# Splitting every second weight tile by DMA and ScalarE, in a two-layer decoder trunk

## The chip, the cores and the metric

The kernel runs on one core of a Trainium2 chip, as one program. The metric is the device time of one execution in microseconds (us), taken as the median over runs.

## The reference

Two residual layers over 256 positions of width 2048, in float32, each behind an RMSNorm, and a final RMSNorm:

```python
def even_mixer(h, w_in, ..., w_out):
    proj = h @ w_in
    ...
    return jnp.concatenate([y_a, y_b], axis=-1) @ w_out

def odd_mixer(h, w_in, ..., w_out, lambda_init):
    proj = h @ w_in
    q, k, v, g = jnp.split(proj, 4, axis=-1)
    ...
    return o @ w_out

def reference(x, norm_w, ..., final_norm_w):
    h = x
    for layer in range(DEPTH):
        hn = rmsnorm(h, norm_w[layer])
        if layer % 2 == 0:
            h = h + even_mixer(hn, ...)
        else:
            h = h + odd_mixer(hn, ...)
    return rmsnorm(h, final_norm_w)
```

In layer 0 the projection feeds a state-space scan (y_a) and a gated mixing of positions (y_b); in layer 1 it feeds differential attention with a gate.

Four weight matrices make nearly all of the work: the input projections of both layers (2048 x 12320 and 2048 x 16384) and their output projections (4096 x 2048 each).

## The kernel before, in words

The matrices lie in memory as tiles of 128 partitions x 2048 float32 (1 MB), in the order of their use. TensorE multiplies in float32r, a float32 with fewer bits, so each float32 operand is kept as a high part (the value as float32r) and a low part (the rest), and a product is made of three: high by high, high by low, low by high. Activations (`xw`, `ya`, `yb`) are split once. Weights are split as they arrive, in half tiles of 128 x 1024.

The path of a weight tile before: `fetch` (line 122) loads it whole into one of three `raw` buffers, by a DMA that SyncE issues (line 124). `halves` (127) splits it in two by `split` (115): ScalarE copies half of it into a `wh` tile (line 118), VectorE subtracts that from the raw half into a `wl` tile (line 119). The pool `wp` has three buffers for each of `raw`, `wh` and `wl`. Tiles are used in one of two ways. `t_accum` (141), through `t_half` (132), has the weight as the stationary operand: eight pairs of matmuls per half, line 136 with `wh` (512 columns) and line 138 with `wl` (256 columns). `tok_proj` (157) has it as the moving operand: four triples per half, lines 168 (`wh`), 169 (`wl`) and 170 (`wh`). The last block of the last output projection is written out apart (line 529).

Layer 0 goes through eight state-space groups (tiles B, C and two x each, and four z tiles for every two groups), four v blocks of four tiles, and sixteen pairs of u and zb tiles (the gating part). `out_proj` takes two tiles, a and b, for each of 16 blocks; per block ScalarE copies half the sum out of PSUM (`sm`), squares the result (`sq`), and POOL adds the square to a running sum `sqa` (line 545). Layer 1 goes eight times through eight q and k tiles, four v and four g tiles, with scores and attention between; POOL's row for `rr_h` (line 177) stands once per head.

The program is written in this order, and a planner with a cost table of its own then puts the instructions of each engine into a fixed sequence; an engine executes its sequence strictly in order, and an instruction that waits holds up all behind it. The first two tiles are fetched and split apart from the others (`first_half`, `split_first`). POOL issues a few transfers of its own: constants at the start and, in the gating part, four times the tiles `lw`, `lb`, `ws_j` and `sb_j` of 256 KB (lines 472 to 486).

Of the kernel before, what the change touches and what calls it, by code (L numbers as in the profile page):

```python
# [9 lines left out]
F32 = mybir.dt.float32  # L10
F32R = mybir.dt.float32r
AF = mybir.ActivationFunctionType
ALU = mybir.AluOpType
AX = mybir.AxisListType
# [3 lines left out]
P = 128  # L18
S = 256
D = 2048  # L20
KB = D // P
EPS = 1e-6
# [6 lines left out]


def order_l0():
    """Weight tiles of the first projection, in the order of their use."""
    out = []
    for gp in range(4):
        for g in (2 * gp, 2 * gp + 1):
            out.append(("T", 4096 + g * P))
            out.append(("T", 5120 + g * P))
            out.append(("T", 2048 + 2 * g * P))
            out.append(("T", 2048 + (2 * g + 1) * P))
        for kq in range(4):  # L40
            out.append(("K", gp * 512, kq))
    for vg in range(4):
        for kq in range(4):
            out.append(("K", 10272 + vg * 512, kq))
    for j in range(16):
        out.append(("T", 8224 + j * P))
        out.append(("T", 6176 + j * P))
    return out
# [24 lines left out]
def hybrid_trunk(ctx: ExitStack, tc: tile.TileContext, xT, cols, dskip, dtp, lnw, lnb, sgub, wsT,  # L73
                 wdt, w0, wo0, w1, wo1, outT):
    nc = tc.nc
    v, act, pe, pool = nc.vector, nc.scalar, nc.tensor, nc.gpsimd

    const = ctx.enter_context(tc.tile_pool(name="const", bufs=1))
    wp = ctx.enter_context(tc.tile_pool(name="wp", bufs=3))
    ev = ctx.enter_context(tc.tile_pool(name="ev", bufs=2))  # L80
    big = ctx.enter_context(tc.tile_pool(name="big", bufs=1))
    acc_p = ctx.enter_context(tc.tile_pool(name="acc_p", bufs=4, space=PSUM))
# [3 lines left out]
    def aux(name):  # L86
        return aux_p.tile([P, 512], F32, tag="aux", name=name)

# [1 line left out]
    col = const.tile([P, N_COLS], F32, name="col")  # L90
    act.dma_start(col, cols)
    ident = const.tile([P, P], F32, name="ident")
# [16 lines left out]
    def c1(i):  # L109
        return col[:, i:i + 1]  # L110

# [1 line left out]
    last_split = [None, None]  # L113

    def split(raw, shape, nm):
        wh = wp.tile([P] + shape, F32R, tag="wh", name=f"wh_{nm}")
        wl = wp.tile([P] + shape, F32R, tag="wl", name=f"wl_{nm}")
        last_split[0] = act.activation(wh, raw, AF.Copy).ins  # L118
        last_split[1] = v.tensor_tensor(wl, raw, wh.bitcast(F32), op=ALU.subtract).ins  # L119
        return wh, wl  # L120

    def fetch(src, nm):
        raw = wp.tile([P, 2048], F32, tag="raw", name=f"raw_{nm}")
        nc.sync.dma_start(raw, src)
        return raw

    def halves(src, inner, nm):
        raw = fetch(src, nm).rearrange("p (a b) -> p a b", b=inner)
        n = 2048 // inner // 2
        return [split(raw[:, h * n:(h + 1) * n, :], [n, inner], f"{nm}_{h}") for h in range(2)]  # L130

    def t_half(ps, hv, x, half, first, last):
        wh, wl = hv
# [5 lines left out]
                      start=False, stop=last and k == 15)  # L139

    def t_accum(ps, src, x, first, last, nm):
        """ps[:, :256] += wh.xh ; ps[:, 256:] += wh.xl + wl.xh, over 16 blocks of k."""
        hv = halves(src, P, nm)
        for half in range(2):
            t_half(ps, hv[half], x, half, first, last)
# [25 lines left out]
        return ps  # L171

    def pow_mhalf(dst, ssum, n, scale, nm):
        """dst = (ssum * scale + EPS) ** -0.5 for [P, n]."""
        ms = ev.tile([P, 2], F32, tag="ms", name=f"ms_{nm}")
        v.tensor_scalar(ms[:, :n], ssum, scale, EPS, op0=ALU.mult, op1=ALU.add)
        pool.tensor_tensor(dst, ms[:, :n], mhalf[:, :n], op=ALU.pow)

    def token_rstd(sqs, nm, copy=True):
        """From sums of squares by channel-partition [P, S], in parts: rstd by token, as columns and as rows."""  # L180
        pcs = [aux(f"pc{tb}_{nm}") for tb in range(2)]
        ms = ev.tile([P, 2], F32, tag="ms", name=f"ms_{nm}")
        for tb in range(2):
            for i, sq in enumerate(sqs):
                pe.matmul(pcs[tb][:, 0:1], lhsT=sq[:, tb * P:(tb + 1) * P], rhs=ones[:, 0:1],
                          start=i == 0, stop=i == len(sqs) - 1)
            v.tensor_scalar(ms[:, tb:tb + 1], pcs[tb][:, 0:1], 1.0 / D, EPS, op0=ALU.mult, op1=ALU.add)
        rt = const.tile([P, 2], F32, tag="rt", name=f"rt_{nm}", bufs=2)
        pool.tensor_tensor(rt, ms, mhalf, op=ALU.pow)
        pb = aux(f"pb_{nm}")  # L190
        for tb in range(2):
            pe.matmul(pb[:, tb * P:(tb + 1) * P], lhsT=rt[:, tb:tb + 1].broadcast_to([P, P]),
                      rhs=ident, start=True, stop=True)
        if not copy:
            return rt, pb[:, 0:S]
        rb = const.tile([P, S], F32, tag="rb", name=f"rb_{nm}", bufs=1)
        act.activation(rb, pb[:, 0:S], AF.Copy)
        return rt, rb

    def put_split(dst, src, scale):  # L200
        """dst [P, 2, S] = hi and lo part of src * scale."""
        act.activation(dst[:, 0, :], src, AF.Copy, scale=scale)
        v.scalar_tensor_tensor(dst[:, 1, :], src, scale, dst[:, 0, :].bitcast(F32),
                               op0=ALU.mult, op1=ALU.subtract)

    # ================= layer 0 =================
    with ExitStack() as l0:
        s1 = l0.enter_context(tc.tile_pool(name="ssd1", bufs=1))

        sqs = s1.tile([P, S], F32, name="sqs")  # L210
        # the first two weight tiles come in halves, between the parts of x
        first = [[None, [None, None]] for _ in range(2)]

        def first_half(i, half):
            if half == 0:
                first[i][0] = wp.tile([P, 2048], F32, tag="raw", name=f"raw_first{i}")
            nc.sync.dma_start(first[i][0][:, half * 1024:(half + 1) * 1024], w0[i][:, half * 1024:(half + 1) * 1024])

        def split_first(i, half):
            raw = first[i][0][:, half * 1024:(half + 1) * 1024].rearrange("p (a b) -> p a b", b=P)  # L220
            first[i][1][half] = split(raw, [8, P], f"first{i}_{half}")

        with tc.tile_pool(name="start", bufs=4) as st:
# [35 lines left out]
            pool.tensor_tensor(sqs, sq[:, 0, 0, :], sq[:, 0, 1, :], op=ALU.add)  # L259
            rt0, rb0 = token_rstd([sqs], "n0")  # L260

            # dt and its cumulative decay
            H = 32
            lo = s1.tile([H, 512], F32, name="dt_lo")
            act.activation(lo, pdt[32:64, :], AF.Copy)
# [9 lines left out]
            e = s1.tile(tok, F32, name="dt_e")  # L275
            q = s1.tile(tok, F32, name="dt_q")
# [5 lines left out]
                                       op0=ALU.mult, op1=ALU.add)  # L282
            v.scalar_tensor_tensor(e, z, -1.0, z, op0=ALU.mult, op1=ALU.max)
            act.activation(e, e, AF.Exp, scale=-1.0)
            # log(1 + e) = 2 atanh(e / (2 + e)), e in [0, 1]
            v.tensor_scalar(w, e, 2.0, None, op0=ALU.add)
            v.reciprocal(w, w)
            pool.tensor_tensor(w, e, w, op=ALU.mult)
# [58 lines left out]
        def ssd_group(g):  # L347
            n = f"g{g}"
# [23 lines left out]
            for b in range(2):  # L372
                for c in range(2):
# [4 lines left out]
            pool.memset(xd[:, 2 * S:2 * S + 64], 0.0)  # L378
            v.tensor_tensor(xd[:, 0:2 * S].rearrange("p (c r q) -> p c r q", r=4, q=64), heads(xt),
                            bc(dtk[:, :, hs].rearrange("p c (r o) -> p c r o", o=1), [P, 2, 4, 64]), op=ALU.mult)  # L380
            # carried state of chunk 0 and what it adds to chunk 1
            wt = sp.tile([P, 4], F32, tag="wt", name=f"wt_{n}")
            v.tensor_tensor(wt, csb[:, :, P - 1:P].rearrange("p r o -> p (r o)"), csk[:, 0, hs], op=ALU.subtract)
            act.activation(wt, wt, AF.Exp)
# [60 lines left out]
    with ExitStack() as l0b:  # L445
# [10 lines left out]
        v.tensor_reduce(nmu, vs, axis=AX.X, op=ALU.add)  # L456
        v.tensor_scalar(nmu, nmu, -1.0 / D, None, op0=ALU.mult)
        vq = g1.tile([P, 2], F32, name="vq")
        for tb in range(2):
            junk = gp_.tile([P, D], F32, tag="junk", name=f"vjunk{tb}", bufs=1)  # L460
            act.activation(junk, vt[:, tb, :], AF.Square, bias=nmu[:, tb:tb + 1], accum_out=vq[:, tb:tb + 1])
        vr = g1.tile([P, 2], F32, name="vr")
        pow_mhalf(vr, vq, 2, 1.0 / D, "ln")
        ws_t = sb_t = None
        for j in range(16):
            n = f"j{j}"
# [42 lines left out]
            act.activation(yb[:, j, 0, :], mx, AF.Copy)  # L509
            v.tensor_tensor(yb[:, j, 1, :], mx, yb[:, j, 0, :].bitcast(F32), op=ALU.subtract)  # L510

# [1 line left out]
    resp = ctx.enter_context(tc.tile_pool(name="resp", bufs=1, reuse_waits="tile"))  # L513
    res = resp.tile([P, KB, S], F32, name="res")
    sqa = resp.tile([P, S], F32, name="sqa")

    def out_proj(w, nm, after):
        """res += the projection; the sums of squares of res by channel-partition are left in
        two parts: all blocks but the last, and the last."""
        pool.memset(sqa, 0.0)  # L520
        for n in range(16):
            ps = acc(f"{nm}_{n}")
# [27 lines left out]
    sqp = out_proj(wo0, "o0", lambda n: put_split(xw[:, n], res[:, n, :], c1(C_NW1 + n)))  # L550
    rt1, rb1 = token_rstd(sqp, "n1")

    # ================= layer 1 =================
    with ExitStack() as l1:
        ap = l1.enter_context(tc.tile_pool(name="att", bufs=2, reuse_waits="tile"))
        a1 = l1.enter_context(tc.tile_pool(name="att1", bufs=1, reuse_waits="tile"))
# [16 lines left out]
        wi[0] = 0  # L573

        def qk_block(tag, c0, nm):
            """[d, token] in float32, and tokens from c0 on in hi and lo parts."""
            ps = acc(nm)
            t_accum(ps, nxt(w1), xw, True, True, nm)
            t = t_sum(ps, nm)
            o = ap.tile([P, S], F32, tag=tag, name=nm)  # L580
            v.tensor_tensor(o, t, rb1, op=ALU.mult)
            hl = ap.tile([P, 2, S - c0], F32R, tag=tag + "hl", name=f"{nm}_hl")
            act.activation(hl[:, 0, :], o[:, c0:S], AF.Copy)
            v.tensor_tensor(hl[:, 1, :], o[:, c0:S], hl[:, 0, :].bitcast(F32), op=ALU.subtract)
            return o, hl

        def scores(qs, ks, nm):
            """softmax over both maps of one head, combined and turned: attnT [k, q]."""
            e = ap.tile([P, 768], F32, tag="e", name=f"e_{nm}", bufs=1)
            e0 = e[:, 0:256].rearrange("p (j k) -> p j k", k=P)  # L590
            e1 = e[:, 256:768].rearrange("p (j k) -> p j k", k=S)
# [89 lines left out]
    n = 0  # L681
# [70 lines left out]
```

## Time and profile before

| | |
|---|---|
| median of two runs | 1737.49 us (1736.93 and 1738.04) |
| the profiled execution, first to last instruction (span) | 1735.4 us |
| TensorE busy | 1713.9 us, 99% |
| VectorE, ScalarE, POOL busy | 65%, 57%, 6% |
| mean granted TensorE clock | 0.997 of full speed |
| moved by DMA | 318.68 MB, 184 GB/s |

The profiled execution has no time of its own beside its span; it is 1.5 and 2.6 us shorter than the two runs, which also count what lies around the instructions. Engines: PE is TensorE, DVE is VectorE, ACT is ScalarE, POOL is GpSimd, SP is SyncE, which only issues DMAs here. "Busy" of PE counts a matmul from its start to its modelled end, and matmuls overlap: their pace is read from the distance of their starts. A row of waits names the waiting instruction and, behind the arrow, what released it.

### The profile page before, as it was taken

To read this page: it belongs to the slowest core of one execution; us is meant where nothing else is said; L and a number is where in the kernel's file an instruction comes from. 1 tells how busy PE (TensorE), PEld (TensorE's weight loads), DVE (VectorE), ACT (ScalarE), POOL (GpSimd) and SP (SyncE) were. 2 spreads that over 40 slices of the span, in tenths; PEclk is the share of its full clock that TensorE was granted. 3 is DMA by queue.
4 is the path that set the end of the run, shared out by engine and by line. 5 is a ranking of instruction groups with operands and counts; after the bars stand their busy time and mean duration, and the time that the engine had idled before them with its cause. 6 is when DMAs were issued, how large, how long until landed. Compare 5 with 4: busy or idle time off the path is not lost.

```text
span 1735.4 us, 23829 instructions
## 1 busy us (share of the span) xinstructions
PE 1713.9 (99%) x9232; PEld 1465.9 (84%) x9232; DVE 1128.1 (65%) x1704; ACT 989.3 (57%) x1521; POOL 104.6 (6%) x159
## 2 busy tenths in 40 slices
PE   7999999999999999999999999999999999999997
PEld 6888888888888888888888888888888888888886
DVE  6987878545777655556666565756576665655454
ACT  6776776545777744445455555555554555555443
POOL 3200000100000011110000000000000000001111
PEclk9999999999999999999999999999999999999998
DMA  7645444655555565554445444554545455445552
GB/s 251 211 168 192 176 172 154 227 186 205 196 201 175 184 232 191 194 188 176 170 171 190 173 170 173 182 179 170 184 162 189 170 187 178 170 170 194 194 188 104
DMA packets 46290, 318.68 MB, mean 184 GB/s; under 512 B 5280, under 2 KB 5584, under 8 KB 9440
## 3 DMA queue, kind: packets, MB, share of 16 engines
q1 hardware_dynamic: 44400, 310.30, 50.5%
q0 software_dynamic: 1344, 4.24, 0.9%
q10 hardware_dynamic: 432, 2.61, 0.4%
q8 instruction: 72, 1.18, 0.3%
q14 instruction: 42, 0.34, 0.1%
HBM read 315.00 MB, written 2.13 MB: 183 GB/s over the span
## 4 chain that ended last, share of the span: by engine, by line
PE 96%; DVE 1%; issue 1%; POOL 1%; DMA 0%; ACT 0%; SPq 0%; DVEq 0%; POOLq 0%
PE acc_o L136 13%; PE acc_q L136 7%; PE acc_k L136 7%; PE acc_o L138 7%; PE acc_v L168 5%; PE acc_v L170 5%; PE acc_v L169 5%; PE acc_q L138 3%; PE acc_k L138 3%; PE acc_g L169 3%; PE acc_g L168 3%; PE acc_zb L136 3%; PE acc_u L136 3%; PE acc_g L170 3%; PE acc_x L136 3%; PE acc_zb L138 2%
## 5 line engine op out<-in xcount | busy, mean ns | idle before, releaser
L136 PE MATMUL acc_q<-xw,wh_q 128*128 128x512 f32 x512 | 182.9, 394 | 0.0
L136 PE MATMUL acc_k<-xw,wh_k 128*128 128x512 f32 x512 | 181.5, 395 | 0.0
L118 ACT ACTIVATE wh_v<-raw_v 128x1024 fp32r<-128x1024 f32 x96 | 101.8, 1060 | 125.0 <-PE acc_v L170 83.6
L119 DVE TENSOR_TENSOR wl_v<-raw_v,wh_v 128x1024 fp32r<-128x1024 f32 x96 | 117.5, 1224 | 79.9 <-ACT wh_v L118 79.9
L169 PE MATMUL acc_v<-wl_v,xw 128*128 128x512 f32 x384 | 152.2, 396 | 0.0
L170 PE MATMUL acc_v<-wh_v,xw 128*128 128x512 f32 x384 | 152.2, 396 | 0.0
L138 PE MATMUL acc_k<-xw,wl_k 128*128 128x256 f32 x512 | 145.5, 284 | 0.0
L138 PE MATMUL acc_q<-xw,wl_q 128*128 128x256 f32 x512 | 145.2, 284 | 0.0
L168 PE MATMUL acc_v<-wh_v,xw 128*128 128x512 f32 x384 | 140.4, 397 | 0.0
L119 DVE TENSOR_TENSOR wl_g<-raw_g,wh_g 128x1024 fp32r<-128x1024 f32 x64 | 78.5, 1226 | 78.7 <-ACT wh_g L118 78.7
L119 DVE TENSOR_TENSOR wl_q<-raw_q,wh_q 128x1024 fp32r<-128x1024 f32 x64 | 78.4, 1226 | 61.9 <-ACT wh_q L118 61.9
L118 ACT ACTIVATE wh_q<-raw_q 128x1024 fp32r<-128x1024 f32 x64 | 67.8, 1060 | 83.9 <-PE acc_g L170 23.9
L136 PEld LDWEIGHTS acc_k<-xw,wh_k 128*128 128x128 f32 x512 | 96.4, 188 | 21.3
L118 ACT ACTIVATE wh_g<-raw_g 128x1024 fp32r<-128x1024 f32 x64 | 67.8, 1059 | 80.7 <-PE acc_g L170 53.4
L136 PEld LDWEIGHTS acc_q<-xw,wh_q 128*128 128x128 f32 x512 | 96.4, 188 | 20.2
L118 ACT ACTIVATE wh_k<-raw_k 128x1024 fp32r<-128x1024 f32 x64 | 67.6, 1057 | 75.0 <-PE acc_q L136 49.0
L169 PE MATMUL acc_g<-wl_g,xw 128*128 128x512 f32 x256 | 101.4, 396 | 0.0
L170 PE MATMUL acc_g<-wh_g,xw 128*128 128x512 f32 x256 | 101.0, 395 | 0.0
L119 DVE TENSOR_TENSOR wl_k<-raw_k,wh_k 128x1024 fp32r<-128x1024 f32 x64 | 78.1, 1221 | 34.7 <-ACT wh_k L118 34.7
L138 PEld LDWEIGHTS acc_k<-xw,wl_k 128*128 128x128 f32 x512 | 96.0, 188 | 1.2
L138 PEld LDWEIGHTS acc_q<-xw,wl_q 128*128 128x128 f32 x512 | 96.1, 188 | 0.9
L136 PE MATMUL acc_x<-xw,wh_x 128*128 128x512 f32 x256 | 92.2, 399 | 0.0
(500 smaller groups left out, 4635.6 us busy)
## 6 DMA issues: line engine op xcount, KB each, us to landing
raw_v<-in_w_dram SPq DMA_DIRECT2D x48, 1024.0 KB, 4.8
raw_q<-in_w_dram SPq DMA_DIRECT2D x32, 1024.0 KB, 4.7
raw_k<-in_w_dram SPq DMA_DIRECT2D x32, 1024.0 KB, 4.8
raw_g<-in_w_dram SPq DMA_DIRECT2D x32, 1024.0 KB, 4.8
raw_x<-in_w_dram SPq DMA_DIRECT2D x16, 1024.0 KB, 4.8
raw_z<-in_w_dram SPq DMA_DIRECT2D x16, 1024.0 KB, 4.8
raw_u<-in_w_dram SPq DMA_DIRECT2D x16, 1024.0 KB, 4.8
raw_zb<-in_w_dram SPq DMA_DIRECT2D x16, 1024.0 KB, 4.8
```

The source lines that it names most:

```text
L118: last_split[0] = act.activation(wh, raw, AF.Copy).ins
L119: last_split[1] = v.tensor_tensor(wl, raw, wh.bitcast(F32), op=ALU.subtract).ins
L136: pe.matmul(ps, lhsT=wh[:, i, :], rhs=x[:, k, :, :].rearrange("p a b -> p (a b)"), start=first and k == 0, stop=False)
L138: pe.matmul(ps[:, 256:512], lhsT=wl[:, i, :], rhs=x[:, k, 0, :], start=False, stop=last and k == 15)
L168: pe.matmul(ps[tb], lhsT=xh, rhs=wh, start=k == 0, stop=False)
L169: pe.matmul(ps[tb], lhsT=xh, rhs=wl, start=False, stop=False)
L170: pe.matmul(ps[tb], lhsT=xl, rhs=wh, start=False, stop=k == 15)
```

## The change

From the 42nd tile on, every second weight tile takes another path (`split_by_dma`). It is not loaded raw. POOL issues a DMA that writes the high part straight from memory, casting float32 to float32r; ScalarE writes the negative of the high part into the low tile; POOL issues a second DMA that reads the same weights from memory again and adds them to the low tile. VectorE has no part in it. The other tiles keep their path, but are loaded by halves into raw buffers of half the size. `wp` has four buffers for each of `raw`, `wh` and `wl`. Comments are gone, and two squares of 2048 columns are taken in four of 1024.

```diff
-    wp = ctx.enter_context(tc.tile_pool(name="wp", bufs=3))
+    wp = ctx.enter_context(tc.tile_pool(name="wp", bufs=4))
...
+    def split_by_dma(src, inner, nm):
+        shape = [P, 1024 // inner, inner]
+        wh = wp.tile(shape, F32R, tag="wh", name=f"wh_{nm}")
+        wl = wp.tile(shape, F32R, tag="wl", name=f"wl_{nm}")
+        pool.dma_start(wh.rearrange("p a b -> p (a b)"), src)
+        act.activation(wl, wh.bitcast(F32), AF.Copy, scale=-1.0)
+        pool.dma_start(wl.rearrange("p a b -> p (a b)"), src, accum_op=ALU.add)
+        return wh, wl
+
     def fetch(src, nm):
-        raw = wp.tile([P, 2048], F32, tag="raw", name=f"raw_{nm}")
+        raw = wp.tile([P, 1024], F32, tag="raw", name=f"raw_{nm}")
         nc.sync.dma_start(raw, src)
         return raw
 
+    n_tiles = [0]
+
     def halves(src, inner, nm):
-        raw = fetch(src, nm).rearrange("p (a b) -> p a b", b=inner)
-        n = 2048 // inner // 2
-        return [split(raw[:, h * n:(h + 1) * n, :], [n, inner], f"{nm}_{h}") for h in range(2)]
+        n_tiles[0] += 1
+        by_dma = n_tiles[0] > 40 and n_tiles[0] % 2 == 0
+        out = []
+        for h in range(2):
+            part = src[:, h * 1024:(h + 1) * 1024]
+            if by_dma:
+                out.append(split_by_dma(part, inner, f"{nm}_{h}"))
+                continue
+            raw = fetch(part, f"{nm}_{h}").rearrange("p (a b) -> p a b", b=inner)
+            out.append(split(raw, [1024 // inner, inner], f"{nm}_{h}"))
+        return out
...
-            junk = gp_.tile([P, D], F32, tag="junk", name=f"vjunk{tb}", bufs=1)
-            act.activation(junk, vt[:, tb, :], AF.Square, bias=nmu[:, tb:tb + 1], accum_out=vq[:, tb:tb + 1])
+            for h in range(2):
+                junk = gp_.tile([P, 1024], F32, tag="junk", name=f"vjunk{tb}{h}", bufs=1)
+                act.activation(junk, vt[:, tb, h * 1024:(h + 1) * 1024], AF.Square, bias=nmu[:, tb:tb + 1],
+                               accum_out=vqs[:, tb, h:h + 1])
+        v.tensor_reduce(vq, vqs, axis=AX.X, op=ALU.add)
```

In the changed kernel the lines are 128 (casting DMA), 129 (negation), 130 (adding DMA), 118 and 119 (the old split), 157 and 159 (the pair of matmuls), 562 (`sm`), 566 (`sq`) and 568 (`sqa`). The planner makes a new sequence. ScalarE before, in the first output projection, from block 5 on (`wh_o0_5a_0` is the first half of block 5's tile a, `xw` the split of a finished block):

```order
L118 ACTIVATE wh_o0_5a_0_6162<-raw_o0_5a_6160 128x1024 [waits DMAHW5_49,PE_49,Activation_49]
L118 ACTIVATE wh_o0_5a_1_6166<-raw_o0_5a_6160 128x1024 [waits PE_49,Activation_49]
L118 ACTIVATE wh_o0_5b_0_6204<-raw_o0_5b_6202 128x1024 [waits DMAHW6_49,DVE_49,PE_49]
L539 ACTIVATE sm_o0_4_6150<-acc_o0_4_6065 128x256 [waits PE_49]
L118 ACTIVATE wh_o0_5b_1_6208<-raw_o0_5b_6202 128x1024 [waits DVE_49,PE_49]
L543 ACTIVATE sq_o0_4_6154<-res_5685 128x256 [waits DVE_49,Pool_49]
L202 ACTIVATE xw_92<-res_5685,col_75 128x256
L118 ACTIVATE wh_o0_6a_0_6256<-raw_o0_6a_6254 128x1024 [waits DMAHW7_49,PE_49,Activation_49]
```

ScalarE there now, from the negation for block 4's tile b on:

```order
L129 ACTIVATE wl_o0_4b_0_6261<-wh_o0_4b_0_6260 128x1024 [waits DMASW5_49,DMASW6_49,DVE_49,PE_49]
L118 ACTIVATE wh_o0_5a_0_6314<-raw_o0_5a_0_6312 128x1024 [waits DMAHW5_49,DVE_49,PE_49]
L129 ACTIVATE wl_o0_4b_1_6266<-wh_o0_4b_1_6265 128x1024 [waits DMASW7_49,DMASW4_49]
L118 ACTIVATE wh_o0_5a_1_6320<-raw_o0_5a_1_6318 128x1024 [waits DMAHW6_49,PE_49,Activation_49]
L562 ACTIVATE sm_o0_3_6206<-acc_o0_3_6119 128x256 [waits PE_49]
L566 ACTIVATE sq_o0_3_6210<-res_5827 128x256 [waits DVE_49,Pool_49]
L223 ACTIVATE xw_92<-res_5827,col_75 128x256
L129 ACTIVATE wl_o0_5b_0_6357<-wh_o0_5b_0_6356 128x1024 [waits DMASW2_49,PE_49]
L129 ACTIVATE wl_o0_5b_1_6362<-wh_o0_5b_1_6361 128x1024 [waits DMASW0_49,DMASW3_49,PE_49,Activation_49]
L118 ACTIVATE wh_o0_6a_0_6410<-raw_o0_6a_0_6408 128x1024 [waits DMAHW7_49,PE_49,Activation_49]
```

Every high part was a copy that waited for SyncE's load (`DMAHW`) and a free buffer; now the rows for tile b are negations of line 129 that wait for POOL's transfer (`DMASW`), and the copies for the next tile a stand behind them.

POOL had in this place one row per block, the sum of line 545. Of the difference on POOL, the stretch from block 4's tile b to block 5's:

```order
+L128 DMA wh_o0_4b_0_6260<-in_wo0_dram 128x1024 [waits DVE_49,PE_49]
+L128 DMA wh_o0_4b_1_6265<-in_wo0_dram 128x1024 [waits DMASW2_49,PE_49]
+L130 DMA wl_o0_4b_0_6261<-in_wo0_dram 128x1024 [waits Activation_49]
+L130 DMA wl_o0_4b_1_6266<-in_wo0_dram 128x1024 [waits DMASW4_49,PE_49,Activation_49]
+L128 DMA wh_o0_5b_0_6356<-in_wo0_dram 128x1024 [waits DVE_49,PE_49]
+L568 TENSOR_TENSOR sqa_5828<-sqa_5828,sq_o0_3_6210 128x256 [waits Activation_49,Pool_49]
+L128 DMA wh_o0_5b_1_6361<-in_wo0_dram 128x1024 [waits DMASW6_49,DMASW3_49,PE_49]
+L130 DMA wl_o0_5b_0_6357<-in_wo0_dram 128x1024 [waits Activation_49]
+L130 DMA wl_o0_5b_1_6362<-in_wo0_dram 128x1024 [waits DMASW5_49,DMASW0_49,Activation_49]
```

POOL now issues four transfers per tile b; the first high half waits for TensorE to free its buffer, both low halves wait for ScalarE's negation, and the sum of block 3 stands between two high halves.

## Rows read from the trace of the kernel before

**Rows 1.** The page: busy us (share of the span), by engine.

```profile
span 1735.4 us, 23829 instructions
...
PE 1713.9 (99%) x9232; PEld 1465.9 (84%) x9232; DVE 1128.1 (65%) x1704; ACT 989.3 (57%) x1521; POOL 104.6 (6%) x159
```

**Rows 2.** TensorE's waits (us, times, longest us): two of five.

```profile
PE acc_dt L243 <- DVE wd L239: 8.0, 1, 8.0
PE acc_x L138 <- DVE wl_x L119: 2.8, 2, 1.7
```

**Rows 3.** Timeline of TensorE (start us, us), where two tiles meet.

```profile
1254.66 0.39 PE L168 MATMUL acc_g<-wh_g,xw 128*128 128x512 f32 x1
...
1255.35 0.40 PE L136 MATMUL acc_q<-xw,wh_q 128*128 128x512 f32 x1
...
1255.71 0.40 PE L136 MATMUL acc_q<-xw,wh_q 128*128 128x512 f32 x1
```

**Rows 4.** The page: split of a half tile (busy us, mean ns).

```profile
L118 ACT ACTIVATE wh_v<-raw_v 128x1024 fp32r<-128x1024 f32 x96 | 101.8, 1060 | 125.0 <-PE acc_v L170 83.6
L119 DVE TENSOR_TENSOR wl_v<-raw_v,wh_v 128x1024 fp32r<-128x1024 f32 x96 | 117.5, 1224 | 79.9 <-ACT wh_v L118 79.9
```

**Rows 5.** POOL's transfers: KB, median us to landing; extremes (lw, sb_j); one alone.

```profile
lw<-in_lnw_dram POOLq DMA_DIRECT2D x4, 256.0 KB, 4.9
lb<-in_lnb_dram POOLq DMA_DIRECT2D x4, 256.0 KB, 6.0
ws_j<-in_wsT_dram POOLq DMA_DIRECT2D x4, 256.0 KB, 5.5
sb_j<-in_sgub_dram POOLq DMA_DIRECT2D x4, 256.0 KB, 5.6
...
DMA to landing us min/median/max: 3.6/4.9/5.9
...
DMA to landing us min/median/max: 3.4/5.6/8.3
...
439.66 0.54 POOL L482 DMA_DIRECT2D ws_j<-in_wsT_dram  x1 [12.95 <-PE pm_j L501]
443.87 1.16 POOL L483 TENSOR_SCALAR_AFFINE_SELECT ws_j<-ws_j 128x512 f32<-128x512 f32 x1 [3.67 <-DMA ws_j<-in_wsT_dram]
```

**Rows 6.** SyncE's transfers: KB each, median us to landing.

```profile
raw_q<-in_w_dram SPq DMA_DIRECT2D x32, 1024.0 KB, 4.7
csb_g<-csd SPq DMA_DIRECT2D x8, 512.0 KB, 3.6
```

**Rows 7.** Steps of the gating part, layer 1, the output projection.

```profile
L501 PE MATMUL pm_j<-ws_j,vt x64: 270/275/275, 428.7 to 599.0; 128*128 128x128 f32 x64
...
1337.19 0.69 POOL L177 TENSOR_TENSOR rr_h<-ms_h,mhalf 128x2 f32<-128x2 f32 x1 [73.49 <-DVE ms_h L176]
...
1432.71 0.69 POOL L177 TENSOR_TENSOR rr_h<-ms_h,mhalf 128x2 f32<-128x2 f32 x1 [73.50 <-DVE ms_h L176]
...
1693.47 1.41 POOL L545 TENSOR_TENSOR sqa<-sqa,sq_o 128x256 f32<-128x256 f32 x1 [9.76 <-ACT sq_o L543]
1704.64 1.41 POOL L545 TENSOR_TENSOR sqa<-sqa,sq_o 128x256 f32<-128x256 f32 x1 [9.76 <-ACT sq_o L543]
```

**Rows 8.** Windows (us, busy by engine, PEclk, DMA share, GB/s); a stall.

```profile
30.00:40.00 10.00, 8.89 (x53) 7.80 (x54) 7.00 (x10) 2.58 (x4) 3.54 (x7) 1.00 0.60 210
1722.00:1723.00 1.00, 1.00 (x12) 1.00 (x10) 0.08 (x1) 0.00 (x0) 0.00 (x0) 1.00 0.00 0
1725.00:1726.00 1.00, 0.46 (x2) 0.46 (x3) 0.00 (x0) 0.00 (x0) 0.49 (x1) 0.62 0.00 0
1726.00:1727.00 1.00, 0.77 (x4) 0.47 (x3) 0.19 (x1) 0.00 (x0) 0.00 (x0) 0.50 0.00 0
...
31.11 0.38 PE L138 MATMUL acc_x<-xw,wl_x 128*128 128x256 f32 x1 [1.66 <-DVE wl_x L119]
```

**Rows 9.** The page, SyncE's DMA queue: packets, MB, share.

```profile
q1 hardware_dynamic: 44400, 310.30, 50.5%
```

More of the change, by code (lines that the diff above doesn't have):

```diff
@@ L210, in hybrid_trunk @@
         sqs = s1.tile([P, S], F32, name="sqs")
-        first = [[None, [None, None]] for _ in range(2)]
+        first = [[[None, None], [None, None]] for _ in range(2)]
         def first_half(i, half):
-            if half == 0:
-                first[i][0] = wp.tile([P, 2048], F32, tag="raw", name=f"raw_first{i}")
-            nc.sync.dma_start(first[i][0][:, half * 1024:(half + 1) * 1024], w0[i][:, half * 1024:(half + 1) * 1024])
+            first[i][0][half] = fetch(w0[i][:, half * 1024:(half + 1) * 1024], f"first{i}_{half}")
         def split_first(i, half):
-            raw = first[i][0][:, half * 1024:(half + 1) * 1024].rearrange("p (a b) -> p a b", b=P)
+            raw = first[i][0][half].rearrange("p (a b) -> p a b", b=P)
             first[i][1][half] = split(raw, [8, P], f"first{i}_{half}")
@@ L458, in hybrid_trunk @@
         vq = g1.tile([P, 2], F32, name="vq")
+        vqs = g1.tile([P, 2, 2], F32, name="vqs")
         for tb in range(2):
-            junk = gp_.tile([P, D], F32, tag="junk", name=f"vjunk{tb}", bufs=1)
-            act.activation(junk, vt[:, tb, :], AF.Square, bias=nmu[:, tb:tb + 1], accum_out=vq[:, tb:tb + 1])
+            for h in range(2):
[3 more added lines that the diff above has]
+        v.tensor_reduce(vq, vqs, axis=AX.X, op=ALU.add)
         vr = g1.tile([P, 2], F32, name="vr")
```

## The prediction

> **What bounds the kernel now.** I read the page's shares first: TensorE is busy 1713.9 of 1735.4 us, VectorE 65% [rows 1]. The list of what TensorE waited for is next: five waits, the longest 8.0 us in the start-up and 2.8 us for a low part of a weight tile, 13 us together [rows 2]. Nothing that relieves another engine can therefore give back 2% (35 us), about what a measurement of this kernel can tell from no change. The question is only whether the new path delivers its tiles in time.
>
> Its deadline comes from TensorE's pace. A pair of lines 136 and 138 starts every 0.35 us (1255.35 to 1255.71), a triple of lines 168 to 170 every 0.69 us [rows 3]. Half a weight tile (1024 columns) is eight pairs or four triples, so 2.8 us in either kind. Half tiles rotate through four buffers for the high and four for the low part. From the changed tiles on, the four belong in turn to a tile split on VectorE (two halves) and one split by DMA (two halves). When TensorE lets go of a half split by DMA, it has three more halves to do, 3 x 2.8 = 8.4 us, before it needs the next content of that buffer. I call one VectorE tile plus one DMA tile a pair of tiles. It takes 95.52 / 8 = 11.94 us in layer 1 (one POOL row per 16 tiles), 11.17 us in the output projections, and (599.0 - 428.7) / 15 = 11.36 us in the gating part [rows 7].
>
> **The change part by part.** Tiles are counted by the code: of 286 tiles the even ones above 40 go by DMA, 123 tiles or 246 halves: 27 in the rest of layer 0's input projection, 32 in the output projections, 64 in layer 1.
>
> VectorE loses 246 subtractions of 1.224 us [rows 4], 301 us. It ended only 2.8 us of TensorE's waits, so I count 0.
>
> ScalarE makes a negation of 128 x 1024 where it made a copy of 128 x 1024, 1.06 us each [rows 4]: 0 in busy time. But the negation waits in an in-order queue for a DMA. Behind it on ScalarE stand the high part of the next VectorE tile and the PSUM copies, as the order rows show. At 1.06 us each they have room inside the cycle below.
>
> POOL gets 492 transfers. By the order rows a tile's four stand as high 0, high 1, low 0, low 1, and each low part waits for its negation.
>
> The chain per buffer is the cost: TensorE frees the buffer, DMA for the high part, negation, adding DMA for the low part, eight pairs on TensorE, and only then is the buffer free again. No reordering shortens this loop, so a pair of tiles cannot take less than the sum of the four.
>
> - *High part, 512 KB from POOL.* The trace has no such transfer. Sixteen of 256 KB from POOL have medians by tensor of 4.9 to 6.0 us from issue to landing; the quickest are 3.4 and 3.6, the slowest, in a batch of eight, 8.3; one on its own was waited for 3.67 us after its issue of 0.54 [rows 5]. From 512 KB to 1024 KB SyncE's loads go from 3.6 to 4.7 us, so 0.6 us for 256 KB more [rows 6]. That gives 4.8 for a lone transfer and 6.1 for the median. Three transfers of 512 KB and two raw halves share each cycle, so I take 5.5. The bounds are 3.4 and 8.3 + 0.6 = 8.9. Whether casting costs anything no row shows.
> - *Negation:* 1.06.
> - *Low part, adding.* The engine must also read what lies in the tile. That costs between nothing (5.5) and, if the data are handled twice, another 1.2 us (6.7); I take 6.1. If adding runs at a quarter of the rate, 1.2 becomes 4.8 and the leg 9.1.
> - *TensorE's hold:* 2.8 at full clock, 5.6 at half. At the end of the kernel the clock is 1.00 while TensorE is dense, 0.62 from 1725 and 0.50 from 1726; a stall of 1.66 us near the start left it at 1.00 [rows 8]. The new stall is 5.5 + 1.06 + 6.1 - 8.4 = 4.3 us per pair, though the planner puts a half of the next VectorE tile inside it and so cuts it in two. Also, a matmul with the next tile's high part stands before the low-part ones. I take 3.5, nearer to the full clock, as the pieces are nearer to 1.66.
>
> By the Trainium skill (DMA: Bandwidth & Descriptors, "Anatomy of one DMA"), a POOL transfer costs about 2.0 us plus its bytes at 436 GB/s; for 512 KB that gives 3.2 us, an estimate from the page. By it the loop would be 3.2 + 1.06 + 3.2 + 2.8 = 10.3 us and nothing would show. The trace disagrees: half the bytes took 3.4 us at best and 4.9 to 6.0 in the median [rows 5].
>
> The loop is 5.5 + 1.06 + 6.1 + 3.5 = 16.2 us. Over 64 pairs in layer 1: 64 x (16.2 - 11.94) = 273 us. Over 32 in the output projections: 32 x (16.2 - 11.17) = 161. Over the 27 others: 27 x (16.2 - 11.36) = 131. In nine tiles POOL's order is high 0, low 0, high 1, low 1. There the second half starts only after the first low part's issue, at 5.5 + 1.06 + 0.5 = 7.1 us, and is ready at 7.1 + 12.7 = 19.8 instead of 16.2: 9 x 3.6 = 32. Sum 597 us. The profiled execution has a span of 1735.4 us, 2.1 below the runs' median of 1737.49; I add to the median: 1737.5 + 597 = 2335 us.
>
> Two edits cost nothing. Raw tiles by halves leave the first 40 tiles four raw halves: load 3.6 [rows 6], copy 1.06, subtraction 1.22 [rows 4] make 5.9 us against the 11.2 us in which TensorE uses four halves; without that cover each half would show the difference. The two squares cut into four add two instruction starts. Bandwidth: the new path moves 2 MB where 1 MB was moved, 123 times, 129 MB beside 310 MB that took 50.5% of the DMA engines [rows 9], so some 72%. That is not a bound by itself unless adding is several times slower than copying.
>
> **The rivals.**
> *Hidden (not slower).* If both legs land as the quickest 256 KB did [rows 5], in 3.5 us, the loop is 3.5 + 1.06 + 3.5 + 2.8 = 10.9 us, below every pair's time, and the result is 1737 us. It decides at legs of about 3.7 us. For it: rows of 3.4 and 3.6. Against: twice the bytes, the median, and the reading of the destination.
> *Quick legs.* Both legs like a lone transfer, 4.8 us, at full clock: loop 13.5 us; 64 x 1.56 + 32 x 2.33 + 27 x 2.14 = 232, so 1970 us.
> *The clock falls in every cycle.* Hold 5.6, loop 18.3: 64 x 6.36 + 32 x 7.13 + 27 x 6.94 + 32 = 855, so 2590 us. For it: 0.50 soon after TensorE went quiet at the end [rows 8]. Against: 1.00 after a stall of 1.66 us, and stalls that come in pieces. The Trainium skill (TensorE: Matmul & The Clock Gate, "HAM oscillation") tells of a kernel whose wait for a DMA in every tile dropped the clock in every tile; the fall at the end agrees, and no row here shows it between tiles.
> *Adding is slow.* A leg of 9.1: loop 19.2; 64 x 7.26 + 32 x 8.03 + 27 x 7.84 + 32 = 965, so 2700 us. No row speaks for or against; two slow legs of 8.9 would lead further, to about 2900.
> *The cast changes nothing.* If the casting DMA kept all bits, the low part would be zero; the instructions and the time are the same.
>
> **How the numbers follow.** Forecast, with legs a little off either way, 2170 to 2550: 0.42. Quick legs (1800 to 2170): 0.25. Clock: 0.13. Slow adding: 0.15. Hidden: 0.05, of which 0.01 for faster by more than 2%, since TensorE's waits have little to give, and 0.04 for within 2%. All other cases are slower: 0.95. The range from 1900 to 2900 us leaves out the hidden case, the lower quarter of the quick legs and the far end of the slow adding.
>
> **What would show it.** Right: TensorE's share near 75%; its longest waits at line 136 or 138 and 168 or 169 for POOL's DMAs or for ScalarE's copies just behind a negation; POOL's transfers at 5 to 7 us; output projection blocks (the sums on POOL) about 16 us apart; VectorE about 300 us less busy. Wrong: blocks still 11.2 us apart (hidden); stalls elsewhere than at DMA tiles; landings far above 7 us; or a granted clock much below 1.00 in the middle of the kernel, which would move the cost from the legs to the hold.

## The result, and the profile after

The changed kernel takes 2413.36 us (median of 2 runs), the kernel before 1737.49: a ratio of 1.389, 95% interval 1.3867 to 1.3913. Slower, as forecast, by 676 us where 597 were worked out.

The page of the changed kernel, shares and DMA queues:

```profile
span 2409.5 us, 24832 instructions
...
PE 1934.9 (80%) x9232; PEld 1592.2 (66%) x9232; DVE 832.2 (35%) x1459; ACT 980.0 (41%) x1525; POOL 440.9 (18%) x651
...
q0 software_dynamic: 72192, 262.23, 48.8%
q1 hardware_dynamic: 50160, 181.33, 22.3%
```

VectorE lost 296 us [rows 1] and nobody gained by it. Of the 674 us that the span grew, TensorE's idle time took 453 (from 21.5 to 474.6 us) and its busy time 221 (from 1713.9 to 1934.9) for the same 9232 matmuls. The list of what TensorE waited for (us, times, longest us) has DMAs of low parts at its head, where [rows 2] had a start-up wait of 8.0:

```profile
PE acc_v L190 <- DMA wl_v<-in_w_dram: 87.6, 23, 9.7
PE acc_g L190 <- DMA wl_g<-in_w_dram: 73.3, 16, 7.4
PE acc_k L159 <- DMA wl_k<-in_w_dram: 53.2, 21, 3.7
PE acc_zb L159 <- DMA wl_zb<-in_w_dram: 45.4, 20, 6.7
PE acc_q L159 <- DMA wl_q<-in_w_dram: 43.5, 16, 4.0
```

One such wait, on TensorE's timeline in the first output projection (start us, us):

```profile
933.75 0.40 PE L157 MATMUL acc_o<-yb,wh_o_11b 128*128 128x512 f32 x1
934.92 0.50 PE L157 MATMUL acc_o<-ya,wh_o_12a 128*128 128x512 f32 x1 [0.77 <-ACT wh_o_12a L118]
939.56 0.58 PE L159 MATMUL acc_o<-yb,wl_o_11b 128*128 128x256 f32 x1 [4.14 <-DMA wl_o_11b<-in_wo_dram]
939.94 0.63 PE L157 MATMUL acc_o<-yb,wh_o_11b 128*128 128x512 f32 x1
940.37 0.41 PE L159 MATMUL acc_o<-yb,wl_o_11b 128*128 128x256 f32 x1
940.58 0.63 PE L157 MATMUL acc_o<-yb,wh_o_11b 128*128 128x512 f32 x1
```

TensorE stands still for 4.14 us until the adding DMA has landed. After that a pair of matmuls takes 0.64 us (939.94 to 940.58) where [rows 3] had 0.35. Windows before, in and after this stretch, and two of layer 1 (us, busy by engine, PEclk, DMA share, GB/s):

```profile
930.00:934.00 4.00, 3.65 (x20) 3.07 (x20) 0.00 (x0) 2.19 (x3) 0.88 (x1) 1.00 0.44 159
940.00:944.00 4.00, 4.00 (x14) 3.42 (x14) 0.00 (x0) 0.00 (x0) 0.00 (x0) 0.50 0.85 287
946.00:950.00 4.00, 4.00 (x26) 3.52 (x25) 0.00 (x0) 1.13 (x2) 0.04 (x2) 1.00 0.42 127
...
1000.00:1400.00 400.00, 314.80 (x1442) 256.74 (x1441) 122.89 (x231) 143.33 (x245) 69.98 (x99) 0.89 0.73 183
1400.00:1800.00 400.00, 315.06 (x1406) 256.86 (x1405) 123.44 (x228) 149.24 (x251) 69.06 (x97) 0.87 0.72 179
```

The granted clock is 1.00 before the wait, 0.50 after it and 1.00 again from 946 on. Such stretches are the busy time that grew; over layer 1 the mean is 0.87 to 0.89.

The new transfers, from issue to landing (KB each, median us; then for `wh_v` and `wl_v` the extremes):

```profile
wh_v<-in_w_dram POOLq DMA_DIRECT2D x48, 512.0 KB, 4.7
wl_v<-in_w_dram POOLq DMA_DIRECT2D x48, 512.0 KB, 7.8
...
wh_zb<-in_w_dram POOLq DMA_DIRECT2D x32, 512.0 KB, 5.4
wl_zb<-in_w_dram POOLq DMA_DIRECT2D x32, 512.0 KB, 8.2
```

```profile
DMA to landing us min/median/max: 3.9/4.7/9.6
DMA to landing us min/median/max: 6.3/7.8/12.3
```

The steps that answer to [rows 7] are `rr_h` on POOL in layer 1, where every second row is one round of 16 tiles further on; `sqa` in the first output projection, from block 1's sum to block 4's; and, in the gating part, the first and last matmul of `acc_zb` (first the kernel after, then before), since the planner moved `pm_j`:

```profile
1276.23 0.71 POOL L198 TENSOR_TENSOR rr_h<-ms_h,mhalf 128x2 f32<-128x2 f32 x1 [2.85 <-DVE ms_h L197]
...
1416.31 0.71 POOL L198 TENSOR_TENSOR rr_h<-ms_h,mhalf 128x2 f32<-128x2 f32 x1 [2.78 <-DVE ms_h L197]
```

```profile
798.89 0.75 POOL L568 TENSOR_TENSOR sqa<-sqa,sq_o 128x256 f32<-128x256 f32 x1
...
848.02 0.75 POOL L568 TENSOR_TENSOR sqa<-sqa,sq_o 128x256 f32<-128x256 f32 x1
```

```profile
L157 PE MATMUL acc_zb<-xw,wh_zb x256: 387/397/633, 480.7 to 749.3; 128*128 128x512 f32 x128
```

```profile
L136 PE MATMUL acc_zb<-xw,wh_zb x256: 388/396/476, 417.3 to 598.3; 128*128 128x512 f32 x128
```

A pair of tiles now takes 140.1 / 8 = 17.5 us in layer 1 and 49.1 / 3 = 16.4 in the output projection. In the gating part the ratio 268.6 / 181.0 takes 11.36 to 16.9. 64 x (17.5 - 11.94) + 32 x (16.4 - 11.17) + 27 x (16.9 - 11.36) = 356 + 167 + 150 = 673 us: the whole loss is in the pace of the pairs with a DMA tile. (Eleven of the 27 lie ahead of the gating part and are counted at its pace.)

### The profile page after: what moved, and what is told of

Its sections match the earlier page's. It is cut to its first block, busy times and chain, and to the rows that moved or that the text cites. A ratio compares the mean times of both kernels' runs of the same rounds, so it can differ in the third digit from the quotient of the medians.

```text
span 2409.5 us, 24832 instructions
## 1 busy us (share of the span) xinstructions
PE 1934.9 (80%) x9232; PEld 1592.2 (66%) x9232; DVE 832.2 (35%) x1459; ACT 980.0 (41%) x1525; POOL 440.9 (18%) x651
## 3 DMA queue, kind: packets, MB, share of 16 engines
q0 software_dynamic: 72192, 262.23, 48.8%
q1 hardware_dynamic: 50160, 181.33, 22.3%
## 4 chain that ended last, share of the span: by engine, by line
issue 40%; PE 24%; DMA 23%; POOL 7%; ACT 3%; DVE 2%; POOLq 0%; SPq 0%; DVEq 0%; ACTq 0%
DMA wl_v<-in_w_dram 3%; DMA wh_v<-in_w_dram 2%; DMA wl_g<-in_w_dram 2%; DMA wl_q<-in_w_dram 2%; PE acc_o L157 2%; PE acc_x L157 2%; PE acc_o L159 1%; PE acc_v L190 1%; DMA wh_q<-in_w_dram 1%; PE acc_q L157 1%; PE acc_v L191 1%; PE acc_B L157 1%; DMA wl_zb<-in_w_dram 1%; PE acc_C L157 1%; PE acc_x L159 1%
## 5 line engine op out<-in xcount | busy, mean ns | idle before, releaser
L157 PE MATMUL acc_k<-xw,wh_k 128*128 128x512 f32 x512 | 209.7, 439 | 6.1 <-ACT wh_k L118 6.0
L190 PEld LDWEIGHTS acc_v<-wl_v,xw 128*128 128x128 f32 x384 | 79.1, 206 | 115.5 <-issue 72.4
L159 PE MATMUL acc_zb<-xw,wl_zb 128*128 128x256 f32 x256 | 81.4, 318 | 45.5 <-DMA wl_zb<-in_w_dram 45.4
L190 PEld LDWEIGHTS acc_g<-wl_g,xw 128*128 128x128 f32 x256 | 54.5, 213 | 92.4 <-issue 51.7
L191 PE MATMUL acc_g<-wh_g,xw 128*128 128x512 f32 x256 | 113.0, 441 | 0.0
L157 PE MATMUL acc_zb<-xw,wh_zb 128*128 128x512 f32 x256 | 105.7, 441 | 0.0
L189 PE MATMUL acc_g<-wh_g,xw 128*128 128x512 f32 x256 | 103.6, 438 | 0.0
L129 ACT ACTIVATE wl_q<-wh_q 128x1024 fp32r<-128x1024 f32 x32 | 33.9, 1059 | 165.1 <-DMA wh_q<-in_w_dram 163.2
L119 DVE TENSOR_TENSOR wl_v<-raw_v,wh_v 128x1024 fp32r<-128x1024 f32 x48 | 57.9, 1223 | 122.5 <-ACT wh_v L118 121.5
L157 PE MATMUL acc_u<-xw,wh_u 128*128 128x512 f32 x256 | 95.6, 406 | 3.9 <-ACT wh_u L118 3.8
L129 ACT ACTIVATE wl_v<-wh_v 128x1024 fp32r<-128x1024 f32 x48 | 50.7, 1056 | 107.9 <-DMA wh_v<-in_w_dram 107.8
```

The source lines that it names most:

```text
L129: act.activation(wl, wh.bitcast(F32), AF.Copy, scale=-1.0)
L157: pe.matmul(ps, lhsT=wh[:, i, :], rhs=x[:, k, :, :].rearrange("p a b -> p (a b)"), start=first and k == 0, stop=False)
L159: pe.matmul(ps[:, 256:512], lhsT=wl[:, i, :], rhs=x[:, k, 0, :], start=False, stop=last and k == 15)
L189: pe.matmul(ps[tb], lhsT=xh, rhs=wh, start=k == 0, stop=False)
L190: pe.matmul(ps[tb], lhsT=xh, rhs=wl, start=False, stop=False)
L191: pe.matmul(ps[tb], lhsT=xl, rhs=wh, start=False, stop=k == 15)
```

## The experiments

Twelve kernels, one run each; the kernel before took 1736.7 to 1738.4 us beside them, the changed kernel is the 2413 us above. "Pair" is the mean over the 123 changed pairs, 11.6 (the kernel before, by the paces of [rows 7]) + (time - 1737.5) / 123. Landings are the medians of `wh_v` and `wl_v`. In layer 1 of the changed kernel the medians of the other tensors go from 4.1 to 4.9 us and from 6.6 to 7.6, so these two are on the long side. The POOL columns sum its list of waits: at line 128 for TensorE to free a high buffer, at line 130 for ScalarE, mostly for the negation.

```
kernel                   us    pair   wh    wl   POOL<-PE  POOL<-ACT  clock
as changed              2413   17.1   4.7   7.8     918       662     0.904
no adding               2135   14.8   4.9   5.2     738       636     0.943
no raw loads            2248   15.8   4.0   6.6     895       512     0.927
five buffers            2201   15.4   7.3   7.2     587       726     0.948
five, no adding         1913   13.0   6.6   4.7     365       749     0.982
five, no raw loads      1954   13.4   5.1   6.5     508       548     0.985
six high, no raw loads  1924   13.1   6.6   7.1     258       753     0.989
six high                2204   15.4  10.2   6.7     106      1208     0.947
```

**Raw tiles by halves alone.**

```
-        by_dma = n_tiles[0] > 40 and n_tiles[0] % 2 == 0
+        by_dma = False
```

> The change without its DMA split: all tiles keep the copy on ScalarE and the subtraction on VectorE, with raw halves and four buffers of each kind. Theory (the time is lost in the loop of a buffer: casting DMA, negation, adding DMA, TensorE): 1737 us within 10, TensorE 99% busy. Rival (raw halves or the buffers themselves cost something): above 1770 us.

1742.21 us, TensorE 99% busy. Halves, the fourth buffers and the cut squares cost some 5 us together; the new path is the rest.

**The second transfer copies.**

```
-        pool.dma_start(wl..., src, accum_op=ALU.add)
+        pool.dma_start(wl..., src)
```

> The second DMA copies (and casts) in place of adding, with the same waits before and behind it; the low part then holds the weight itself, so the part of the computation that the low weights make is changed. Theory: the second leg falls from 7.7 to about 4.9 us, the loop by 2.8, and with fewer stalls the clock falls less often: 1950 to 2120 us, middle 2030. Rival (the number of transfers, their bytes from memory, or POOL's in-order queue set the time): 2300 us or more.

2135.14 us, just above the expected stretch. Adding alone costs 278 of the 676 us; two plain legs in the same loop still cost 398. Its queue line, beside the 48.8% of 2409.5 us above:

```profile
span 2133.3 us, 24832 instructions
...
q0 software_dynamic: 72192, 262.23, 38.8%
```

So POOL's transfers held the 16 DMA engines for 828 us, with adding for 1176, by the same packets and bytes. For the two transfers of one half (there are 246) that is 3.36 and 4.78 us.

**Only the high part by DMA**, the low part by VectorE from a raw half.

```
         pool.dma_start(wh..., src)
-        act.activation(wl, wh.bitcast(F32), AF.Copy, scale=-1.0)
-        pool.dma_start(wl..., src, accum_op=ALU.add)
+        raw = fetch(src, nm)...
+        v.tensor_tensor(wl, raw, wh.bitcast(F32), op=ALU.subtract)
```

> High part by POOL's casting DMA, low part by VectorE from a raw half that SyncE loads; no negation, no adding DMA. Theory: the loop is 4.7 + 1.2 + 2.8 = 8.7 us, below the 11.2 us of a pair of tiles, so 1735 to 1765 us. Rival (transfers issued by POOL, or ScalarE and POOL waiting in order, cost in themselves): above 1850 us.

1790.3 us, 25 above the expected stretch and far from the rival: one POOL leg in the chain is nearly hidden, two in sequence are not.

```profile
span 1788.6 us, 24680 instructions
...
q0 software_dynamic: 36768, 133.24, 21.7%
```

**Five buffers** for each part (paid for by two raw halves instead of four).

```
-        raw = wp.tile(..., tag="raw")      wh, wl = wp.tile(..., tag="wh"), ...
+        raw = wp.tile(..., bufs=2)         wh, wl = wp.tile(..., bufs=5), ...
```

> The change with five buffers for high and low parts in place of four, and two raw halves in place of four (the same memory). Theory: a loop of 16.3 to 17.2 us is now shared by five halves and not four, so a pair of tiles takes 13.0 to 13.8 us: 1737 + 123 x (1.3 to 2.0), 1900 to 2000 us. The two raw halves cost the first 40 tiles some 10 us. Rival (the adding DMA's rate or bandwidth is the bound): 2350 us or more.

2201.42 us, a miss of 200. The fifth buffer gave 212 us, but the high parts landed in 7.3 us instead of 4.7. A landing counts from the issue, so the likeliest reading is that a transfer issued earlier queues behind those in flight.

**Quarters**: pieces of 512 columns, ten buffers for each part, four raw pieces; and the same without the DMA split.

```
-        shape = [P, 1024 // inner, inner]        for h in range(2):
+        shape = [P, 512 // inner, inner]         for h in range(4):
```

> The change in pieces of 512 columns: ten buffers of 256 KB each for high and low parts and four raw ones, the same memory, twice the instructions and transfers. Theory: a loop of about 4.1 + 0.6 + 6 + 1.4 = 12 us (256 KB legs) is shared by ten quarters, which are 14 us of TensorE's work: hidden, 1740 to 1850 us. Rival (rate of adding, bandwidth or POOL's issue are the bound; transfers of 256 KB are less efficient): 2200 us or more.

> Pieces of 512 columns and ten buffers, but no DMA split at all: the price of the smaller pieces alone. All theories: 1737 us within 20.

2196.84 us: a miss, and close to the rival of a limit in the transfers. 1751.55 without the DMA split, so the smaller pieces cost little by themselves. A quarter's high part (256 KB) landed in 7.9 us, later than a half in the changed kernel. Ten quarters hold as many columns as five halves, and the two runs differ by 5 us (2196.84 and 2201.42).

**Filler matmuls**, eight on each DMA half, to keep TensorE from going quiet.

```
+            for j in range(8):
+                pe.matmul(fill, lhsT=wh[:, i, :], rhs=x[:, k], start=True, stop=True)
```

> The change with eight extra matmuls of 512 columns into an unused bank behind the first matmul of each half split by DMA (1.9 us each time, so TensorE is busy in most of the stall). The output is the same. Theory (legs set the loop, the fallen clock lengthens TensorE's part of it): granted clock back to 0.97 or more, loop 16.4 us, 2250 to 2360 us in spite of the added work. Rival 1 (the clock's fall costs nothing, since only legs count): 2413 us or more. Rival 2 (the clock costs all of the 221 us by which TensorE's busy time grew): about 2190 us.

2457.68 us at a clock of 0.975: a miss, on the side of the rival that says the fall of the clock costs nothing. The clock came back and the time did not, though TensorE's idle time fell from 475 to 208 us. The fillers can also lengthen TensorE's hold, by some 1.9 us per half, and hide a gain, so the run says that the clock is not the first cause; it does not price it.

**Five buffers, no adding**: the two edits above together.

> Five buffers for the high and five for the low parts, and the second transfer copies instead of adding (the low part is then the whole weight, so the sums differ from the reference). With four buffers the copy gave 2135 us, with five the adding kernel 2201. Theory of two stacked limits (the loop of buffers, and the time of the shared DMA engines): the loop with the landings of the copy run is (4.9 + 1.06 + 4.7 + 2.8) x 4/5 = 10.8 us, and the engines' time 2 x 3.36 + 2 x 1.55 = 9.8 us for a pair of tiles, both under the 11.2 to 11.9 us of TensorE; at a full load the landings grow somewhat, so 1740 to 1880 us. Rival, a serial limit of its own in POOL's or ScalarE's in-order queue, which neither buffers nor a quicker second leg removes: 2000 us or more.

1912.58 us: between the two. Both edits help and neither is the whole.

**No raw loads after tile 40**, with four buffers and with five.

```
-            raw = fetch(part, f"{nm}_{h}")...
+            if n_tiles[0] <= 40:
+                kept[h] = fetch(part, f"{nm}_{h}")
+            raw = kept[h]...
```

> Four buffers, adding as in the changed kernel, but SyncE loads no raw halves after tile 40: the tiles that VectorE splits are split again and again from the last raw halves loaded (their weights are wrong from there on). Theory of shared DMA engines: a pair of tiles needs 2 x 4.78 = 9.6 us of their time instead of 12.7, so the landings shorten, to about 4.0 for the high and 5.8 for the low part: loop 4.0 + 1.06 + 5.8 + 3.0 = 13.9 us, and 123 x (13.9 - 11.5) = 295 us over before, so 1950 to 2150 us. Rival, POOL's transfers are slow by themselves and do not feel SyncE's: landings as they were and 2380 to 2420 us.

> Five buffers, adding, and no raw halves loaded after tile 40 (VectorE's tiles are split from old raw halves, their weights are wrong). Theory of two stacked limits: loop 13.9 x 4/5 = 11.1 us and engines' time 9.6 us, both under TensorE's 11.2 to 11.9 us: 1740 to 1880 us, with low parts landing in under 6.5 us. Rival, the adding transfers are limited by themselves in POOL's queue: near the 2201 us of five buffers with the raw loads, 2100 us or more.

2248.02 us and 1953.59 us: each some 75 to 100 us above its expected stretch, and below its rival. Without SyncE's loads the low parts land in 6.6 us (four buffers):

```profile
wh_v<-in_w_dram POOLq DMA_DIRECT2D x48, 512.0 KB, 4.0
wl_v<-in_w_dram POOLq DMA_DIRECT2D x48, 512.0 KB, 6.6
```

So the raw loads are worth 0.7 and 1.2 us of the two legs, 165 us in all, and the adding leg stays slow without them (the copy, beside the raw loads, took 5.2). My sums lacked about 1 us per loop: with high + 1.06 + low + 1.0 + 2.8, times 4 / buffers, the first six rows of the table come to 17.4, 15.0, 15.5, 15.5, 12.9 and 13.2 us, within 0.3 of the measured pairs. The 1.0 was fitted to these runs; no row names it (issues and handovers between three engines are where it would lie). The landings are each run's own, so the sum says that a buffer spends its round in these steps and in little else. It does not say why a landing is long; that the loop is the limit rests on what the other runs gave back.

**Six buffers for the high parts**, four for the low, two raw halves; without and with the raw loads.

```
-        wh = wp.tile(shape, F32R, tag="wh", ...)
+        wh = wp.tile(shape, F32R, tag="wh", ..., bufs=6)
```

> Six buffers for the high parts, four for the low ones, two raw halves, adding; no raw halves loaded after tile 40 (VectorE's tiles are split from old raw halves, their weights are wrong). The runs so far fit one sum: (landing of the high part + 1.06 + landing of the low part + about 1 us for issues and handovers + 2.8 of TensorE) x 4 / buffers for a pair of tiles. Theory that this loop is the whole cost as long as the DMA engines have room: high parts (5.5 + 1.06 + 6.6 + 1 + 2.8) x 4/6 = 11.3 us, low parts, whose buffer waits only for the negation, 1.06 + 6.6 + 1 + 2.8 = 11.5 us, beside TensorE's 11.2 to 11.9: 1740 to 1810 us. Rival, a serial limit in POOL's or ScalarE's order, which a longer rotation does not remove: 1900 us or more.

> The same buffers (six high, four low, two raw halves) with all raw halves loaded, so everything is computed as in the changed kernel. By the loop alone, with the landings of the run with five buffers, (7.2 + 1.06 + 7.1 + 1 + 2.8) x 4/6 = 12.8 us for a pair of tiles, so 1737 + 123 x 1.3 = about 1900 us (1870 to 1930). Theory that the time of the 16 DMA engines is a second floor: 2 x 4.78 + 2 x 1.55 = 12.7 us of it for a pair, and at the busy shares of 0.85 to 0.9 seen at most 14.1 to 14.9 us, so 2050 to 2160 us, with landings of the high parts longer than 8 us.

1923.6 us, which is the rival's side, and 2204.32, above both theories. Beside the runs with five buffers for each part, six high and four low ones gave 30 us and nothing; the sum above would give 12.4 and 14.5 us for them instead of 13.1 and 15.4. So the rotation of the high parts had stopped being the limit. For the four low ones the same sum gives 1.06 + 6.7 + 1.0 + 2.8 = 11.6 us, under the 15.4, but six high with five low was not run. POOL's timeline in the last run, and the negation on ScalarE inside it:

```profile
1308.11 0.89 POOL L128 DMA_DIRECT2D wh_g<-in_w_dram  x1
1310.03 0.55 POOL L128 DMA_DIRECT2D wh_g<-in_w_dram  x1 [1.03 <-PE acc_g L191]
1319.06 0.88 POOL L130 DMA_DIRECT2D wl_g<-in_w_dram  x1 [8.48 <-ACT wl_g L129]
1321.59 0.87 POOL L130 DMA_DIRECT2D wl_g<-in_w_dram  x1 [1.66 <-ACT wl_g L129]
1322.14 0.88 POOL L128 DMA_DIRECT2D wh_q<-in_w_dram  x1
...
1317.70 1.06 ACT L129 ACTIVATE wl_g<-wh_g 128x1024 fp32r<-128x1024 f32 x1 [8.54 <-PE acc_g L190]
```

The next tile's first high half (1322.14) has no wait of its own: its buffer was free, but it stands behind the low halves in POOL's order, and the first of them waits 8.48 us for a negation. That negation starts at 1317.70, 0.1 us after the landing of its high half (issued at 1308.11, landed 9.5 us later); its row names a matmul of TensorE, which ended in the same 0.1 us. The second half's landing takes 10.1 us. POOL goes round in 14.0 us (1308.11 to 1322.14). The four transfers from 1305.09 to 1310.03 land after 6.5, 7.6, 9.5 and 10.1 us, at 1311.6, 1315.2, 1317.6 and 1320.1, one behind another, which reads as if the high halves also waited for the low ones ahead of them in the DMA engines. What POOL's order costs apart from that load, these runs do not separate. The same list of waits in the two kernels, changed and with six high buffers, shows POOL's waiting change place:

```profile
POOL wh_v L128 <- PE acc_v L191: 148.1, 34, 9.5
POOL wl_v L130 <- ACT wl_v L129: 139.8, 45, 7.6
```

```profile
POOL wl_v L130 <- ACT wl_v L129: 237.6, 40, 11.9
...
POOL wh_v L128 <- PE acc_v L191: 13.2, 12, 2.2
```

In the changed kernel POOL waits for TensorE to free buffers, 918 us; with six, 106 us, and 1208 us at line 130 for ScalarE (954 of them put down to a negation, the others to ScalarE's rows around it).

## Why the prediction was right, and where its terms were off

*TensorE bound, nothing to gain:* right. VectorE's 296 us came to nothing. TensorE's share, expected near 75%, was 80%: matmuls at half clock count as busy for longer.

*The loop through four buffers sets the pace:* right. Forecast 16.2 us a pair, measured 17.5, 16.4 and 16.9. Shortening one leg (no adding, no raw loads) or lengthening the rotation (five) each gave back a large part, and the loop with each run's own landings and the fitted 1 us gives those times. With six high buffers the sum no longer holds and another limit takes over; it was not the one of the changed kernel.

*High leg, 5.5 us:* too long; 4.7 in the median of `wh_v`, 4.0 without the raw loads. *Low leg, 6.1:* too short; 7.8. The term that was mis-sized is the price of adding, "between nothing and 1.2 us": with the copy in its place the leg takes 5.2, so adding costs 2.6 (by `wl_zb`, 8.2 and 4.5, even 3.7), more than the 1.2 for data handled twice and short of the slow rival's leg of 9.1. Without the raw loads the leg is still 6.6, so they are not the reason for most of it.

The Trainium skill (DMA: Bandwidth & Descriptors, "Anatomy of one DMA") gives 3.2 us for 512 KB by its formula, an estimate from the page. The trace disagrees, though by less than the 5.5 that I took: the quickest `wh_v` took 3.9 us, the median 4.7 here and 4.0 with the raw loads gone.

*TensorE's hold, 3.5:* a little too long. 221 us more busy time over 123 pairs is 1.8 us for four halves, so a half takes 2.8 + 0.45 = 3.25 if all four share it alike. The clock falls after waits and comes back: a consequence of the stalls, and far from the rival's 5.6.

*Sum of the loop:* 4.7 + 1.06 + 7.8 + 3.25 = 16.8 in layer 1, where 17.5 was measured. For the 0.7 us left over (more by the shorter medians of the other tensors) I had no term, and no row names it. That the total came out near is partly luck: the legs' errors (-0.8 and +1.7) partly cancelled, and the 32 us for nine tiles stood in for part of the rest. The pairs were put at 565 us and cost 673.

*Nine tiles in the other POOL order, 32 us:* no run shows this cost. Layer 1 has seven of them; POOL's step from such a tile to the next took 16.1 us in the mean, from the other tiles 17.7.

*Raw halves and squares, 0:* 5 us.

*Bandwidth, "some 72%" and "not a bound by itself":* wrong, though the measured share looks the same (0.72 and 0.73 in the windows of layer 1). The 72% was reckoned by bytes on the span of before, 1241 us of the 16 engines' time. The two queues held them for 48.8% and 22.3% of 2409.5 us, 1713 us, which is 99% of the span of before; that the shares agree is chance. The prediction allowed for a bound only with adding several times slower than copying; twice was enough. Below saturation the load still lengthened both legs, 165 us of the loss. What the bytes miss is that adding takes 4.78 - 1.6 = 3.1 to 3.2 us of the engines per half, where a casting copy takes 1.6 (the kernel with only high parts by DMA: 21.7% of 1788.6 us over 246).

*The far end of the range:* two legs of 8.9 us come, by the prediction's own sum, to some 3060 us and not to "about 2900".

*Open:* a pair asks 2 x 4.78 for POOL's halves and 2 x 1.5 for the raw ones (50.5% of 1735.4 us [rows 9] over 310 MB in halves of 0.524), some 12.6 us of all 16 engines, more than TensorE's 11.2 to 11.9. By this estimate no number of buffers could have hidden the new path. But the changed kernel, at 16.4 to 17.5 us a pair, is not at this floor, and no run reached it: quarters came nearest, with 82.7% of their span on the two queues. Whether another order on POOL (the next tile's high halves ahead of this one's low halves) would get there was not tried. No version beat the kernel before.

## What to carry to other kernels

Before work is moved from an engine with slack to DMA, write down the loop of one buffer: every landing, hop and hold between two releases, times the share of the buffers. It has to be shorter than what the bound engine needs for the rotation, and landings must be taken under the load that the change itself adds. Then add up the time of the DMA engines for a round by kind of transfer, not by bytes: an adding one cost twice a copying one here. When more buffers stop helping, look also at the queue that issues the transfers: an in-order engine that waits between two dependent transfers is a loop of its own. Here that was seen in POOL's waits; no run with another order tested it.

## What the runs showed that I had not expected

- An adding DMA held the DMA engines about twice as long as a casting copy of the same bytes (3.1 against 1.6 us per 512 KB), with the same packets on the queue, and longer on POOL: 0.88 us of issue where the copy in its place takes 0.53.
- More buffers made landings longer: `wh_v` 4.7, 7.3 and 10.2 us with four, five and six, at nearly the same 2201 and 2204 us for the last two.
- One wait of 4.14 us, with one matmul and a wait of 0.77 us just ahead of it, was followed by half clock, where the 1.66 us of [rows 8] was not.
